# First loads on one DMA queue in pieces, the first attention's tables loaded in its first stage, the lambda vectors moved into the attention

## The chip, the cores and the metric

The kernel runs on one core of a Trainium2 chip, in one launch. Its time is device microseconds (us) of that core; the value that counts is the median of several runs. The engines are PE (matrix products, and PEld, its weight loads), DVE (vector), ACT (activation), POOL (GpSimd) and SP, which here only issues DMA transfers. Every engine works through its own instructions in order.

## What is computed

Two layers of a streaming encoder on 1024 tokens of width 1024, in float32. Layer 0 mixes tokens by latent attention, layer 1 by differential attention; each is followed by a normalisation and a SwiGLU block. The change touches the start of layer 0 and one scalar of layer 1:

```python
h = x @ w_in                                   # 1024 x 704: 384 + 256 + 64 columns
c_q, c_kv, k_rope = jnp.split(h, [384, 640], axis=-1)
c_q, c_kv = _rmsnorm(c_q, g_q), _rmsnorm(c_kv, g_kv)
q  = (c_q  @ w_uq ).reshape(b, s, 8, 128 + 64) # 8 heads: plain part, rotary part
kv = (c_kv @ w_ukv).reshape(b, s, 8, 128 + 128)
q_rope, k_rope = rope(q[..., 128:]), rope(k_rope)
logits = (q_nope . k_nope + q_rope . k_rope) * scale, masked by chunks of 64
o = softmax(logits) @ v
...
lam = exp(sum(lam_q1 * lam_k1)) - exp(sum(lam_q2 * lam_k2)) + lambda_init   # layer 1
o   = rmsnorm(o, g_sub) * (1 - lambda_init)                                 # layer 1
```

## The kernel before

**Precision.** Every matrix product is made of three passes on two rounded parts of each operand: hi x hi, hi x lo and lo x hi. So each operand that is loaded is first split: ACT copies it to the type float32r (the hi part, `A.copy`), and DVE or POOL subtracts that from the original (the lo part).

**First stage (pool a0).** `load_x(tb)` loads block tb of x, transposed, 128 x 1024 (512 KB), and splits it into xh and xl; `load_w_in(k)` does the same for rows k of the input weights, 128 x 704 (352 KB), into wih and wil, the lo part on DVE, or on POOL for k = 3, 5, 7. Block 0 of x comes in four pieces, block 1 in two, and the weights whole, in the order x 0, w 0, w 1, x 1, w 2 to w 7. `project` (L960) then multiplies blocks 0 and 1 together, k by k, six pairs of matmuls for each k: L970 writes hq (384 columns, the query latent) and L971 hk (320 columns, the key and value latent and the rotary key). Blocks 2 to 7 follow one at a time, three pairs for each k; there are three buffers for x, xh and xl, so a block's load waits for the block three before. `latents` (L974) squares and normalises a block (cve, crs, cn; it needs the gains gq and gk and the rotary table kt), and `turn_c` transposes cn on PE with the identity ident and splits it into c, ck_hi and ck_lo.

**Queues.** ident, x, the weights and all later loads are issued by SP and go to DMA queue q1. The rows gq and gk, the table kt, the vector g_sub and the four lambda vectors (each spread over 128 partitions by `bcast_row`) are issued by POOL and go to queue q0, at the beginning of the program.

**Lambda.** Behind the first stage, L1019 to L1032 scale g_sub and form the scalar nlam from the four vectors, in a small pool of its own, lam. Both are read by layer 1 only.

**First attention (pools a1...).** The tables ba (the mask), cos and sin, each 128 x 1024 (512 KB), are loaded when these pools open (L1040 to L1045). `q_rope`, `q_nope`, `k_nope` and `values` project two heads' rotary queries (qr), one head's queries (qn) and keys (kn) and two heads' values (v); `q_rope` multiplies its result by cos (L1059, qra) and by sin in four quarters (L1061, qrb), adds both on POOL (L1062) and splits the sum (ACT L1065, L1067; DVE L1066, L1068). `score_a` makes the scores s_a of a block of 128 queries in five passes (L217: three with kn and q, two with ck and the rotary queries) and DVE takes the row maximum (L220, mx_a). `attention` runs head by head and block by block; `at(slot, fn)` hangs a projection or a load on a block's slot.

**Order.** The program is written with pools and tiles, and a scheduler puts each engine's instructions into an order of its own before the kernel is built, by its own estimate of when each can run. So an instruction's place need not be that of its line.

## Time and profile before

Times of the kernel before, in us:

| | |
|---|---|
| median of 3 runs | 2333.69 |
| lowest and highest run | 2331.33, 2339.92 |
| span of the profiled execution | 2331.5 |
| first matmul of the program | 13.47 |
| first matmul of block 2 | 32.07 |
| first matmul of the attention's projections | 82.95 |
| PE busy, share of the span | 2254.7, 97% |

The profile gives no time of its own for the profiled execution beside its span, which lies within the range of the runs; nothing else is added to it. A row of a timeline has the start, the duration, the engine, the line of the kernel, the operation, the names that are written and read, the shape, a count where several are merged, and in brackets the idle time before it with what ended it. "hq L970 <- ACT wih L137: 13.5, 1, 13.5" is a wait: who waited, for whom, us in total, how often, the longest.

### The profile page before, as it was taken

How to read it: one execution, taken by the hardware profiler on the slowest of the kernel's cores; microseconds unless marked ns; L12 is line 12 of the kernel's file. 1: busy time of each engine (PE TensorE's matmuls, PEld its weight loads, DVE VectorE, ACT ScalarE, POOL GpSimd, SP SyncE). 2: the span in 40 equal slices, each digit the busy share in tenths (PEclk: the TensorE clock that was granted, in tenths of full speed). 3: DMA queues.
4: the chain of work that ended last, by engine and by line, in shares of the span. 5: the costliest groups of instructions: out<-in, count | busy, mean ns of one | idle time of the engine just before them, and what ended most of it. 6: DMA issues, size and time to landing. Idle time of an engine off the chain costs nothing. (4 is left out here: it accounts for less than half of the span.)

```text
span 2331.5 us, 31115 instructions
## 1 busy us (share of the span) xinstructions
PE 2254.7 (97%) x11410; PEld 1918.7 (82%) x11410; DVE 1556.9 (67%) x2876; ACT 1017.4 (44%) x2089; POOL 894.8 (38%) x706
## 2 busy tenths in 40 slices
PE   7899999999999999999999999979999999999997
PEld 7898997888888887888888898867788888887885
DVE  4567664596656667677576666666596656658777
ACT  4366664352333333444465656545342333324353
POOL 3233452014444445555432424222014444436564
PEclk9999999999999999999999999989999999999999
DMA  5112324344323238454220212153334323337353
GB/s 201 35 57 89 120 90 161 109 163 153 118 85 131 73 118 320 172 194 153 91 55 19 69 37 69 37 190 101 124 141 151 107 98 106 111 131 303 142 203 118
DMA packets 102490, 288.29 MB, mean 124 GB/s; under 512 B 7856, under 2 KB 30000, under 8 KB 91840
## 3 DMA queue, kind: packets, MB, share of 16 engines
q1 hardware_dynamic: 96480, 267.48, 32.4%
q0 software_dynamic: 5856, 18.81, 2.5%
q8 instruction: 90, 1.47, 0.3%
q14 instruction: 64, 0.52, 0.1%
HBM read 205.00 MB, written 77.07 MB: 121 GB/s over the span
## 5 line engine op out<-in xcount | busy, mean ns | idle before, releaser
L470 ACT CAST op_g<-gr 128x512 fp32r<-128x512 f32 x240 | 147.5, 622 | 410.7 <-PE gb L515 228.1
L471 POOL TENSOR_TENSOR op_g<-gr,op_g 128x512 fp32r<-128x512 f32 x104 | 145.9, 1408 | 303.0 <-DVE tmp L606 153.6
L471 DVE TENSOR_TENSOR op_h<-rh,op_h 128x512 fp32r<-128x512 f32 x154 | 161.4, 1078 | 69.9 <-ACT op_h L470 69.9
L515 PE MATMUL ga<-xh_m,op_g 128*128 128x512 f32 x512 | 168.0, 389 | 0.0
L470 ACT CAST op_h<-rh 128x512 fp32r<-128x512 f32 x154 | 92.9, 619 | 147.7 <-PE dx L783 37.2
L783 PE MATMUL dw<-op_w_t,op_h 128*128 128x512 f32 x660 | 151.4, 390 | 0.2 <-DVE op_h L471 0.2
L783 PEld LDWEIGHTS dw<-op_w_t,op_h 128*128 128x128 f32 x660 | 123.6, 188 | 26.1 <-DVE op_h L471 0.6
L223 ACT ACTIVATE l_b<-l_b,mx_b 128x256 f32<-128x256 f32 (+7 forms) x128 | 99.6, 778 | 76.0 <-DVE mx_b L220 74.3
L1269 POOL TENSOR_SCALAR l_b<-l_b,r_b,cst 128x128 f32<-128x128 f32 (+3 forms) x64 | 52.8, 825 | 204.0 <-DVE r_b L225 194.8
L471 POOL TENSOR_TENSOR op_w_t<-tt,op_w_t 128x512 fp32r<-128x512 f32 x66 | 98.7, 1499 | 78.7 <-ACT op_w_t L470 76.8
L783 PE MATMUL dx<-op_w_b,op_h 128*128 128x512 f32 x528 | 122.6, 391 | 5.9 <-ACT op_w_b L470 3.9
L783 PEld LDWEIGHTS dx<-op_w_b,op_h 128*128 128x128 f32 x528 | 98.4, 188 | 29.8 <-ACT op_w_b L470 4.7
L515 PE MATMUL gb<-t4h_f,op_g 128*128 128x512 f32 x352 | 115.8, 390 | 3.2 <-DVE tmp L598 3.2
L515 PE MATMUL gc<-b22h_f,op_g 128*128 128x512 f32 x352 | 115.6, 389 | 1.0 <-ACT op_g L470 1.0
L471 DVE TENSOR_TENSOR op_g<-gr,op_g 128x512 fp32r<-128x512 f32 x136 | 109.5, 806 | 9.0 <-ACT op_g L470 8.8
L515 PE MATMUL gc<-t1h_f,op_g 128*128 128x512 f32 x352 | 115.5, 389 | 0.0
L515 PE MATMUL gb<-t3h_f,op_g 128*128 128x512 f32 x352 | 115.2, 389 | 0.0
L515 PE MATMUL gb<-t2h_f,op_g 128*128 128x512 f32 x352 | 114.9, 389 | 0.0
L515 PEld LDWEIGHTS ga<-xh_m,op_g 128*128 128x128 f32 x512 | 96.1, 188 | 20.0
L471 POOL TENSOR_TENSOR op_g<-s,op_g 128x512 fp32r<-128x512 f32 x40 | 55.9, 1398 | 142.9 <-ACT op_g L470 142.9
L144 PE MATMUL bp<-xT_f,h_wb 128*128 128x512 f32 x256 | 103.0, 402 | 0.1
L146 PE MATMUL bp<-xT_f,l_wb 128*128 128x512 f32 x256 | 101.6, 397 | 0.0
(381 smaller groups left out, 6788.5 us busy)
## 6 DMA issues: line engine op xcount, KB each, us to landing
gr<-in_w_gu SPq DMA_DIRECT2D x44, 1024.0 KB, 6.6
rh<-h_dr SPq DMA_DIRECT2D x28, 1024.0 KB, 4.9
h_dr<-sh SPq DMA_DIRECT2D x22, 1024.0 KB, 4.9
h_dr<-hp SPq DMA_DIRECT2D x22, 768.0 KB, 4.1
tt<-in_w_dn SPq DMA_DIRECT2D x22, 512.0 KB, 7.6
rh<-h_dr SPq DMA_DIRECT2D x14, 768.0 KB, 4.4
z<-xs_dr SPq DMA_DIRECT2D x16, 512.0 KB, 10.0
rw_b<-in_w_dn SPq DMA_DIRECT2D x8, 1024.0 KB, 8.8
```

What stands on the lines that cost most here:

```text
L144: T.matmul(ps_out, lh, rh, start=(i == 0), stop=False)
L146: T.matmul(ps_out, ll, rh, start=False, stop=(i == n - 1))
L223: A.activation(l[:, :n], l[:, :n], AF.Exp, bias=mx, scale=-1.0, accum_out=sm)
L470: A.copy(hi, src)
L471: eng.tensor_tensor(lo, src, f32(hi), ALU.subtract)
L515: T.matmul(o, w[:, a, kc], x[b][:, k, :], start=(first and k == 0 and (a, b) == (0, 0)), stop=(k == 3 and a == 1), skip_group_check=True,)
L783: T.matmul(o, h[:, a, c], w[:, b_], start=(first and (a, b_) == (0, 0)), stop=(last and a == 1), skip_group_check=True,)
L1269: G.tensor_scalar(l1[:, :n], l1[:, :n], r1, nlam, ALU.mult, ALU.mult)
```

## The change

- The loads of x for blocks 0 and 1 and of the weights are issued in the order in which PE uses them: a quarter of x 0, w 0 in two parts (384 and 320 columns), a quarter of x 1, w 1, and then for each further quarter the pieces of x 0 and x 1 and two weights. `load_x` takes the number of the piece. The weights have five raw buffers instead of eight, and are split within `load_w_in`.
- ident, gq, gk and kt are issued by SP behind these loads. POOL issues no DMA at the start any more.
- The tiles ba, cos and sin move to the pool krp, which is open from the beginning, and are loaded when block 3's x is.
- The lambda vectors and their dot products get room in the tile `edge` (before, it was unused there). Their loads and that of g_sub (`load_late`) are hung on slot 10 of the first attention and the arithmetic (`make_late`) on slot 12.

The sums, the splits and the matmuls are the same; two pieces of a weight are now split in two instructions, and x 1 in four instead of two.

The scheduler sets where these end up. On SP, the first issues of the program (x_0 and x_1 are blocks 0 and 1 of x, wraw0 to wraw7 the weights by k) stood so before:

```order
L102 DMA ident_61<-in_c_ident 128x128
L937 DMA x_0_113<-in_xt 128x256 x4
L133 DMA wraw0_130<-in_w_in_a 128x704
L133 DMA wraw1_136<-in_w_in_a 128x704
L937 DMA x_1_140<-in_xt 128x512 x2
L133 DMA wraw2_151<-in_w_in_a 128x704
L133 DMA wraw3_157<-in_w_in_a 128x704
L133 DMA wraw4_163<-in_w_in_a 128x704
```

and stand so now:

```order
L940 DMA x_0_117<-in_xt 128x256
L949 DMA wraw0_123<-in_w_in_a 128x384
L949 DMA wraw0_123<-in_w_in_a 128x320
L940 DMA x_1_132<-in_xt 128x256
L949 DMA wraw1_138<-in_w_in_a 128x704
L940 DMA x_0_117<-in_xt 128x256
L940 DMA x_1_132<-in_xt 128x256
L949 DMA wraw2_150<-in_w_in_a 128x704
L949 DMA wraw3_156<-in_w_in_a 128x704
```

The first weights stood behind ident and four pieces of x and now stand behind one piece, and half of them counts as a load of its own. Behind these rows come the other pieces of x, w 4 to w 7, ident, gq, gk, kt, x 2, cos, sin, x 3, ba and x 4, then the first attention's first weights, g_sub and the four lambda vectors (places 30 to 34) and x 5 to x 7: although the lambda vectors are written into slot 10 of the attention, the scheduler has put them into the first stage, their arithmetic too, on DVE behind the split of x 4.

On DVE, at the end of the first stage and the start of the attention (c11 and ck_lo are the lo parts of the last block's latents, ql0_0 and kn1_0 those of head 0's first queries and keys, vl0_0 and vl0_1 of the first values, qra0_0 and qrb0_0 the rotary products of the first half, qr0_0 and qr1_0 their lo parts) stood before:

```order
L1004 TENSOR_TENSOR c11_104<-cp7_0_863,c01_102 128x4x128
L1004 TENSOR_TENSOR ck_lo_109<-cp7_4_870,ck_hi_108 128x2x128
L1097 TENSOR_TENSOR ql0_0_964<-qn0_0_953,qh0_0_963 128x512
L1111 TENSOR_TENSOR kn1_0_968<-kn0_0_969,kn0_0_967 128x512
L1083 TENSOR_TENSOR vl0_0_1034<-v0_0_1026,vh0_0_1033 128x256
L1059 TENSOR_TENSOR qra0_0_933<-qr0_0_923,cos_913 128x512
L1083 TENSOR_TENSOR vl0_1_1045<-v0_1_1037,vh0_1_1044 128x256
L1061 TENSOR_TENSOR qrb0_0_934<-qr0_0_923,sin_915 32x512 x4
L1097 TENSOR_TENSOR ql0_1_1083<-qn0_1_1072,qh0_1_1082 128x512
L1066 TENSOR_TENSOR qr0_0_0_941<-qra0_0_933,qr0_0_0_941 64x512
L1068 TENSOR_TENSOR qr1_0_0_942<-qra0_0_933,qr1_0_0_942 64x512
```

and stand now:

```order
L1069 TENSOR_TENSOR qra0_0_920<-qr0_0_910,cos_110 128x512
L1071 TENSOR_TENSOR qrb0_0_921<-qr0_0_910,sin_111 32x512 x4
L1013 TENSOR_TENSOR c11_103<-cp7_0_878,c01_101 128x4x128
L1013 TENSOR_TENSOR ck_lo_108<-cp7_4_885,ck_hi_107 128x2x128
L1107 TENSOR_TENSOR ql0_0_951<-qn0_0_940,qh0_0_950 128x512
L1121 TENSOR_TENSOR kn1_0_955<-kn0_0_956,kn0_0_954 128x512
L1076 TENSOR_TENSOR qr0_0_0_928<-qra0_0_920,qr0_0_0_928 64x512
L1078 TENSOR_TENSOR qr1_0_0_929<-qra0_0_920,qr1_0_0_929 64x512
L1093 TENSOR_TENSOR vl0_0_1021<-v0_0_1013,vh0_0_1020 128x256
L1093 TENSOR_TENSOR vl0_1_1032<-v0_1_1024,vh0_1_1031 128x256
```

The two rotary products moved from behind the first values to the front, ahead of the last block's split, and the lo parts of the rotary queries to the place before the values. PE's order moved with it: the first values now stand ahead of the first scores; the rotary passes of the scores of query blocks 0 and 1 stand behind the rotary projection of the second half, and all passes of block 2 behind that half's keys; before, both came only behind head 1's first query projection. From block 3's scores on PE's order is the old one, but for a few neighbours that change places much later.

```diff
--- before.py
+++ after.py
@@ -83,7 +83,7 @@
     ones = cp.tile([P, P], F32, tag="ones", name="ones")
     cst = cp.tile([P, 48], F32, tag="cst", name="cst")
     edge = ctx.enter_context(tc.tile_pool(name="edge", bufs=1, side="right"))
-    edge.tile([P, 504], F32, tag="edge", name="edge")
+    late = edge.tile([P, 504], F32, tag="edge", name="edge")
     wp = ctx.enter_context(tc.tile_pool(name="wp", bufs=3))
     big = ctx.enter_context(tc.tile_pool(name="big", bufs=5))
     ps, ps_bufs, ps_stack = None, None, None
@@ -99,7 +99,6 @@
     banks("ps0", PS_BUFS_A)
     dr = ctx.enter_context(tc.tile_pool(name="dr", bufs=1, space=DRAM))
 
-    nc.sync.dma_start(ident, c_ident)
     mhalf = cst[:, 0:2]
     V.memset(mhalf, -0.5)
     eps_rms = cst[:, 8:9]
@@ -148,9 +147,9 @@
     def tr(ps_out, in_):
         T.transpose(ps_out, in_, ident)
 
-    def bcast_row(pool, src, n, name, tag):
+    def bcast_row(pool, src, n, name, tag, eng=None):
         t = pool.tile([P, n], F32, tag=tag, name=name, bufs=1)
-        nc.gpsimd.dma_start(t, src.partition_broadcast(P))
+        (eng or nc.gpsimd).dma_start(t, src.partition_broadcast(P))
         return t
 
     def behind(i, j):
@@ -917,6 +916,7 @@
     krp = ast.enter_context(tc.tile_pool(name="krp", bufs=1))
     lat2 = [big_tile("ck_hi"), krp.tile([P, 2, S], F32R, tag="cklo", name="ck_lo")]
     kr1, kr2 = lat2[0][:, 1], lat2[1][:, 1]
+    ba, cos, sin = (krp.tile([P, S], F32, tag=t, name=t) for t in ("ba", "cos", "sin"))
 
     def lat(p, k, t0, n):
 
@@ -927,35 +927,44 @@
     with tc.tile_pool(name="a0", bufs=2, side="right") as pool:
         xs, win = {}, []
 
-        def load_x(tb, n=1):
-
-            xt = pool.tile([P, D], F32, tag="x", name=f"x_{tb}", bufs=3)
-            xh = pool.tile([P, D], F32R, tag="xh", name=f"xh{tb}", bufs=3)
-            xl = pool.tile([P, D], F32R, tag="xl", name=f"xl{tb}", bufs=3)
-            for i in range(n):
-                c = slice(i * D // n, (i + 1) * D // n)
-                nc.sync.dma_start(xt[:, c], xt_in[tb, :, c])
-                A.copy(xh[:, c], xt[:, c])
-                V.tensor_tensor(xl[:, c], xt[:, c], f32(xh[:, c]), ALU.subtract)
-            xs[tb] = (xh, xl)
+        def load_x(tb, i=0, n=1):
+
+            if tb not in xs:
+                xs[tb] = (
+                    pool.tile([P, D], F32R, tag="xh", name=f"xh{tb}", bufs=3),
+                    pool.tile([P, D], F32R, tag="xl", name=f"xl{tb}", bufs=3),
+                    pool.tile([P, D], F32, tag="x", name=f"x_{tb}", bufs=3),
+                )
+            xh, xl, xt = xs[tb]
+            c = slice(i * D // n, (i + 1) * D // n)
+            nc.sync.dma_start(xt[:, c], xt_in[tb, :, c])
+            A.copy(xh[:, c], xt[:, c])
+            V.tensor_tensor(xl[:, c], xt[:, c], f32(xh[:, c]), ALU.subtract)
 
         def load_w_in(k):
             hi = pool.tile([P, 704], F32R, tag=f"wih{k}", name=f"wih{k}", bufs=1)
             lo = pool.tile([P, 704], F32R, tag=f"wil{k}", name=f"wil{k}", bufs=1)
-            raw = pool.tile([P, 704], F32, tag="wraw", name=f"wraw{k}", bufs=8)
-            load_w(w_in_a[k], 704, f"win{k}", hi, lo, G if k > 2 and k % 2 else V, raw)
+            raw = pool.tile([P, 704], F32, tag="wraw", name=f"wraw{k}", bufs=5)
+            for c in (slice(0, 384), slice(384, 704)) if k == 0 else (slice(0, 704),):
+                nc.sync.dma_start(raw[:, c], w_in_a[k][:, c])
+                A.copy(hi[:, c], raw[:, c])
+                (G if k > 2 and k % 2 else V).tensor_tensor(lo[:, c], raw[:, c], f32(hi[:, c]), ALU.subtract)
             win.append((hi, lo))
 
-        load_x(0, 4)
+        load_x(0, 0, 4)
         load_w_in(0)
+        load_x(1, 0, 4)
         load_w_in(1)
-        load_x(1, 2)
-        for k in range(2, KD):
-            load_w_in(k)
-        gq = bcast_row(pool, g_q, RQ, "gq", "gq")
-        gk = bcast_row(pool, g_kv, RKV, "gk", "gk")
+        for i in range(1, 4):
+            load_x(0, i, 4)
+            load_x(1, i, 4)
+            load_w_in(2 * i)
+            load_w_in(2 * i + 1)
+        nc.sync.dma_start(ident, c_ident)
+        gq = bcast_row(pool, g_q, RQ, "gq", "gq", nc.sync)
+        gk = bcast_row(pool, g_kv, RKV, "gk", "gk", nc.sync)
         kt = pool.tile([P, NTB, P], F32, tag="kt", name="kt", bufs=1)
-        nc.gpsimd.dma_start(kt, c_krope)
+        nc.sync.dma_start(kt, c_krope)
 
         def project(tbs):
             ms = [(ps_m(f"hq{tb}"), ps_t(f"hk{tb}")) for tb in tbs]
@@ -963,7 +972,7 @@
                 kc = slice(k * P, (k + 1) * P)
                 wh, wl = win[k]
                 for tb, (hq, hk) in zip(tbs, ms):
-                    xh, xl = xs[tb]
+                    xh, xl, _ = xs[tb]
                     for lh, w, st, sp_ in (
                         (xh, wh, k == 0, False), (xh, wl, False, False), (xl, wh, False, k == KD - 1)
                     ):
@@ -1008,6 +1017,9 @@
             for tb in tbs:
                 if tb > 1:
                     load_x(tb)
+                if tb == 3:
+                    for t, src in ((cos, c_cos), (sin, c_sin), (ba, c_bias_a)):
+                        nc.sync.dma_start(t, src)
             ms = project(tbs)
             for tb, cn in done:
                 turn_c(tb, cn)
@@ -1017,13 +1029,18 @@
 
 
     gs = cst[:, 16:17]
-    nc.gpsimd.dma_start(gs, g_sub)
-    V.tensor_scalar(gs, gs, 1.0 - LAMBDA_INIT, None, ALU.mult)
+    nlam = cst[:, 24:25]
     V.memset(ones, 1.0 / P)
-    nlam = cst[:, 24:25]
-    with tc.tile_pool(name="lam", bufs=1) as pool:
-        lv = [bcast_row(pool, t, 64, f"lv{i}", f"lv{i}") for i, t in enumerate((lam_q1, lam_k1, lam_q2, lam_k2))]
-        dots = pool.tile([P, 2], F32, tag="dots", name="dots")
+    lv = [late[:, 64 * i:64 * i + 64] for i in range(4)]
+    dots = late[:, 256:258]
+
+    def load_late():
+        nc.sync.dma_start(gs, g_sub)
+        for t, src in zip(lv, (lam_q1, lam_k1, lam_q2, lam_k2)):
+            nc.sync.dma_start(t, src.partition_broadcast(P))
+
+    def make_late():
+        V.tensor_scalar(gs, gs, 1.0 - LAMBDA_INIT, None, ALU.mult)
         for i in range(2):
             V.tensor_tensor(lv[2 * i], lv[2 * i], lv[2 * i + 1], ALU.mult)
             V.tensor_reduce(dots[:, i:i + 1], lv[2 * i], mybir.AxisListType.X, ALU.add)
@@ -1031,18 +1048,11 @@
         V.tensor_tensor(nlam, dots[:, 1:2], dots[:, 0:1], ALU.subtract)
         V.tensor_scalar(nlam, nlam, -LAMBDA_INIT, None, ALU.add)
 
-
     with ast as st:
         pool = st.enter_context(tc.tile_pool(name="a1", bufs=2, reuse_waits="tile"))
         vp = st.enter_context(tc.tile_pool(name="a1v", bufs=12, side="right", reuse_waits="tile"))
         lp = st.enter_context(tc.tile_pool(name="a1l", bufs=4, side="right", reuse_waits="tile"))
         ptp = st.enter_context(tc.tile_pool(name="a1p", bufs=5, side="right", reuse_waits="tile"))
-        ba = pool.tile([P, S], F32, tag="ba", name="ba", bufs=1)
-        nc.sync.dma_start(ba, c_bias_a)
-        cos = pool.tile([P, S], F32, tag="cos", name="cos", bufs=1)
-        nc.sync.dma_start(cos, c_cos)
-        sin = pool.tile([P, S], F32, tag="sin", name="sin", bufs=1)
-        nc.sync.dma_start(sin, c_sin)
         vt, qr, qn, kn, wts, lt, pts = {}, {}, {}, {}, {}, {}, {}
 
         def q_rope(pr, hf):
@@ -1163,6 +1173,8 @@
             at(b + (6 if h < H - 1 else 4), q_nope, h, 1)
             at(b + (7 if h < H - 1 else 5), k_nope, h, 1)
         at(8 * H - 20, split_wo, H - 1)
+        at(10, load_late)
+        at(12, make_late)
         attention(score_a, turn_a, mix_a, fill, 2, (0, 0))
 
     banks("ps2", PS_BUFS)
```

## The prediction

> **What bounds the kernel now.** I read the page first, for what the span is made of.
>
> ```profile
> span 2331.5 us, 31115 instructions
> PE 2254.7 (97%) x11410; PEld 1918.7 (82%) x11410; DVE 1556.9 (67%) x2876; ACT 1017.4 (44%) x2089; POOL 894.8 (38%) x706
> ```
>
> PE, the matmul engine, is busy 97% of the span: time can only be won where PE stands still or where its clock is low, 77 us in all. The change works in the first attention's first stage (latents) and at its start, so I cut that stretch into stages, by busy time per engine: before the first matmul; the projection of blocks 0 and 1; blocks 2 to 7; the start of the attention. After the time of each engine come the granted clock, the DMA share and GB/s.
>
> ```profile
> 0.00:13.47 13.47, 0.00 (x1) 0.00 (x1) 1.96 (x8) 3.68 (x6) 4.62 (x12) 1.00 0.79 226
> 13.47:32.07 18.60, 18.60 (x97) 18.17 (x97) 11.33 (x15) 10.31 (x15) 9.31 (x5) 1.00 0.73 277
> 32.07:82.26 50.19, 50.19 (x326) 50.09 (x325) 24.64 (x80) 15.99 (x46) 6.37 (x8) 1.00 0.20 70
> 82.26:112.31 30.05, 24.14 (x116) 19.39 (x116) 20.88 (x47) 13.07 (x31) 8.81 (x8) 0.94 0.20 68
> ```
>
> PE has two holes: 13.47 us at the start and 30.05 - 24.14 = 5.91 us at the transition, where the clock also falls to 0.94. Between them, from 13.47 to 82.26, there is none: whatever is won at the start is carried through to 82.26. The waits of PE up to 125 us name who ended each hole.
>
> ```profile
> PE hq L970 <- ACT wih L137: 13.5, 1, 13.5
> PE s_a L217 <- DVE mx_a L220: 4.2, 3, 2.8
> PE s_a L217 <- ACT kn L1110: 1.7, 1, 1.7
> ```
>
> **The start.** The timeline from 0, SP's DMA issues, ACT and PE:
>
> ```profile
> 0.73 0.38 SPq L102 DMA_DIRECT2D ident<-in_c_ident  x1
> 1.17 1.85 SPq L937 DMA_DIRECT2D x<-in_xt  x4
> 3.06 1.15 SPq L133 DMA_DIRECT2D wraw<-in_w_in_a  x2
> 3.92 0.40 ACT L938 CAST xh<-x 128x256 fp32r<-128x256 f32 x1 [1.91 <-DMA x<-in_xt]
> 12.64 0.78 ACT L137 CAST wih<-wraw 128x704 fp32r<-128x704 f32 x1 [3.31 <-DMA wraw<-in_w_in_a]
> 13.47 0.69 PE L970 MATMUL hq<-wih,xh 128*128 128x384 f32 x1 [13.47 <-ACT wih L137]
> 19.83 0.34 PE L970 MATMUL hq<-wil,xh 128*128 128x384 f32 x1
> 32.07 0.34 PE L970 MATMUL hq<-wih,xh 128*128 128x384 f32 x1
> ```
>
> The first quarter of x is there at 3.92, the first weights only at 12.64. The DMA issues by line (count, KB, us from issue to landing):
>
> ```profile
> ident<-in_c_ident SPq DMA_DIRECT2D x1, 64.0 KB, 1.8
> x<-in_xt SPq DMA_DIRECT2D x4, 128.0 KB, 5.5
> wraw<-in_w_in_a SPq DMA_DIRECT2D x8, 352.0 KB, 9.5
> ```
>
> The queues from 2 to 6 us, and below the dots from 14 to 22 us (packets, MB, share of 16 engines):
>
> ```profile
> q0 software_dynamic: 90, 0.29, 42.0%
> q1 hardware_dynamic: 459, 0.39, 32.5%
> ...
> q1 hardware_dynamic: 1174, 3.33, 103.5%
> ```
>
> From 2 to 6 us GpSimd's queue q0 (gq, gk, kt, g_sub, the lambda vectors) took more of the engines than SP's q1. Per full engine share q1's rows of 1 KB ran at 0.39 MB / (0.325 x 4 us) = 300 GB/s; later, alone, its rows of 2.8 KB ran at 3.33 MB / 8 us = 416 GB/s.
>
> The change puts ahead of the first matmul only one x piece and the left part of w0. x0's piece is issued where ident was, at 0.73, w0's at 0.73 + 1.85/4 = 1.2. Landing costs between ident's 1.8 us and the 2.75 us of the first x piece (1.17 to 3.92): 3.0 to 4.0 us. The cast of 384 columns lies between 0.40 (256) and 0.78 (704), about 0.5. PE starts at 3.5 to 4.5; I take 4.2, nearer to ident, since q0 is silent now. The far bound is the pieces' median of 5.5 us: 1.2 + 5.5 + 0.5 = 7.2. **First term: 13.47 - 4.2 = 9.3 us**, at worst 6.3.
>
> Is PE then fed? Its 48 pairs of matmuls took 19.83 - 13.47 = 6.36 us for the first 10, slow, then (32.07 - 19.83) / 38 = 0.322 each. The weights of one k serve 6 pairs: 3.8 us slow, 1.93 us later, so k = 7 is reached at 4.2 + 6.36 + 32 x 0.322 = 20.9. SP issues 17 pieces at about 0.5 us (1.85/4, 1.15/2), the last by 9, an estimate. The bytes: 1.05 MB of x at 300 GB/s is 3.5 us, 2.88 MB of weights at 416 is 6.9; from 1.7 on, all is there by 13 to 14, 7 us early. The tightest place is k = 0 and 1, where casts follow the landings closely: I charge 0.3 us. The deeper split of w and the five raw buffers instead of eight ask w5 to w7 to wait for DVE's splits of k = 0 to 2, done by about 9, when SP gets there anyway. Block 2's x comes behind ident, gq, gk and kt, 5.37 MB in all: 1.7 + 3.5 + 4.32/0.416 = 15.6 and a cast of 1.05 (0.40 + 768 columns x 0.38/448), against PE's need at 23.1. Cost nothing; cover 5 us or more. So blocks 0 and 1 end at 4.2 + 6.36 + 38 x 0.322 + 0.3 = 23.1 instead of 32.07: **9.0 us (6.0 to 9.9)**.
>
> The slow first pairs are the clock's: from rows 13.47 and 19.83 they cost 0.636 us each against 0.322. The Trainium skill, "TensorE: Matmul & The Clock Gate", Part 1, What's actually happening, states a free-running window of 3.4 us, so warming takes 3.4 to 6.8 us after a start; this trace's 6.36 fits its long end. By that page the sum would gain up to (6.36 - 3.4) x (1 - 0.322/0.636) = 1.5 us more, an estimate; I keep the row's 6.36.
>
> **Lambda, g_sub and the tables.** The five small loads (0.13 MB) stand at places 30 to 34 of SP's queue, with cos, sin and ba ahead. On DVE eight short instructions now stand behind the split of block 4's x and ahead of the latents of block 2, which can't start before PE ends that block, at 23.1 + 50.19/6 = 31.5. The old trace shows that cover as DVE's idle time:
>
> ```profile
> 32.11 1.23 DVE L939 TENSOR_TENSOR xl<-x,xh 128x1024 fp32r<-128x1024 f32 x1 [6.04 <-PE hq L970]
> ```
>
> The lambda rows need 8.9 MB landed, 1.7 + 3.5 + 7.9/0.416 = 24 us, so 7 us of cover: nothing. Without it, each us of lateness would shift the latents, which PE needs only a block (8.4 us) later.
>
> **The transition.** PE, DVE, POOL, ACT and SP:
>
> ```profile
> 51.45 0.42 SPq L1045 DMA_DIRECT2D sin<-in_c_sin  x1
> 84.69 0.39 PE L145 MATMUL qr<-c,h_wa 128*128 128x512 f32 x1
> 84.91 0.40 PE L146 MATMUL qr<-c,l_wa 128*128 128x512 f32 x1
> 85.82 0.48 DVE L993 SCALAR_TENSOR_TENSOR cn<-hk,crs,gk 128x256 f32<-128x256 f32 x1
> 89.83 0.69 DVE L1004 TENSOR_TENSOR c<-cp,c 128x512 fp32r<-128x512 f32 x1 [3.54 <-ACT c L1003]
> 91.11 0.50 PE L217 MATMUL s_a<-kn,qh 128*128 128x128 f32 x2 [1.71 <-ACT kn L1110]
> 91.37 0.68 DVE L1111 TENSOR_TENSOR kn<-kn,kn 128x512 fp32r<-128x512 f32 x1
> 93.28 0.68 DVE L1059 TENSOR_TENSOR qra<-qr,cos 128x512 f32<-128x512 f32 x1
> 94.57 2.79 DVE L1061 TENSOR_TENSOR qrb<-qr,sin 32x512 f32<-32x512 f32 x4
> 97.50 1.29 POOL L1062 TENSOR_TENSOR qra<-qra,qrb 128x512 f32<-128x512 f32 x1 [12.94 <-DVE qrb L1061]
> 98.81 0.62 ACT L1065 CAST qr<-qra 64x512 fp32r<-64x512 f32 x1 [0.38 <-POOL qra L1062]
> 99.47 0.69 DVE L1066 TENSOR_TENSOR qr<-qra,qr 64x512 fp32r<-64x512 f32 x1 [0.31 <-ACT qr L1065]
> 104.86 0.79 PE L217 MATMUL s_a<-kn,qh 128*128 128x384 f32 x2 [2.83 <-DVE mx_a L220]
> 108.67 0.27 PE L149 MATMUL pt_a<-ident,l_a 128*128 128x128 f32 x1
> 114.59 0.34 PE L217 MATMUL s_a<-kn,ql 128*128 128x384 f32 x1
> 114.76 0.33 PE L217 MATMUL s_a<-ck_hi,qr 128*128 128x384 f32 x1
> ```
>
> The tables were not late: sin was issued at 51.45, and its product ran at 94.57. What was late is DVE's place for the rotary products: head 0's raw product is complete at 85.3, DVE idles 3.54 us until 89.83, and only at 93.28 does it multiply. In the new order the products (0.68 + 2.79 = 3.47 us) stand just ahead of that c split: they fill the idle time, and the rotary part is ready at about 89.8 + 1.29 + 0.62 + 0.69 = 92.8 on the old clock, behind the k split (92.05), instead of 100. PE's order follows: the first values come ahead of the scores (the hole of 1.71 shrinks to two of about 0.45), the rotary scores of blocks 0 and 1 right behind the second half's rotary projection, and block 2's scores ahead of head 1's projection, so DVE can free the score banks while PE projects; the 2.83 hole goes. With it goes the slow clock behind it: from 104.86 to 108.67 ten matmuls took 3.81 us; at the later spacings (0.17 for 384 columns, 0.22 for 512) they would take 2.0, so 1.8 us. Walking the new order with the old durations, 1.2 us stay: the two halves of the first hole, and about 0.3 on DVE's row maximum of block 3, then behind the second half's rotary split. Sum: 5.91 + 1.8 = 7.7, less 1.2: **second term 6.5 us**. Bounds: 7.7 above; below, a loss of 1.2, if ACT's two casts of 0.62, now ahead of the values' casts, are waited for and nothing else gains.
>
> The rest of the program keeps its order but for three swaps of neighbours. Both gains shift it as a whole, since nothing there waits on an absolute time.
>
> **Sum.** 9.0 + 6.5 = 15.5 us off the profiled 2331.5: 2316.0. The median of the runs, 2333.7, lies 2.2 above that span, so I forecast 2318.2. A measurement of this kernel can tell about 0.5%, 11.7 us, from no change: under 2322.0 is faster.
>
> **Rivals.** *Start only.* PE's new order meets another wait (a score bank, ACT's casts, POOL's split of a 1024-column weight in between) and the transition gains nothing: 2333.7 - 9.0 = 2324.7. For it: PE's program is in order, and one late producer stalls all. Against it: each producer I followed has 0.3 us or more. Chance 0.14.
>
> *The start is fed poorly.* PE starts early, then waits for pieces with its clock low, and keeps only 5 us: 2333.7 - 11.5 = 2322.2, on the border. For it: both queues together moved only (0.29 + 0.39) MB / 4 us = 170 GB/s from 2 to 6 us; were the 1 KB rows to blame and not q0, 3.9 MB would take until 25. Against it: the 300 GB/s per share. Chance 0.13.
>
> *The queue serves pieces one at a time*, the slower side. Each piece would pay ident's 1.8 us, less 0.2 for its own bytes. Block 5's x is the 35th DMA, 9.44 MB in: 0.73 + 35 x 1.6 + 9.44/0.416 + 1.05 = 80.5, against 32.07 + 3 x 8.37 = 57.2 now: 23.3 late, less 6.5, so 2350.5. It decides from 1.1 us a piece on (24.5 + 35 x 1.1 = 57.2 + 6.5, no gain left; 1.5 for slower by 0.5%). Against it: in 14 to 22 us q1 moved nine weight pieces' worth in 8 us. The Trainium skill, "DMA: Bandwidth & Descriptors", section Measured, says to batch DMAs to 1 MiB or more, and Anatomy of one DMA gives 2.0 us of fixed cost each; taken in series that rule would make it slower still, and the 416 GB/s row speaks against taking it so. Chance 0.04.
>
> *It does not do what it says*: the weights' arrival depends on something other than what is queued, and DVE's place was not the hold-up: 2333.7. Chance 0.03.
>
> **Numbers.** The forecast has 0.66. Faster: 0.66 and half of the poorly fed case, 0.72; same: the other half, start only, no effect, 0.24; slower 0.04. Range: down to 9.9 + 7.7 + 1.5 = 19.1 (2314.6) and 2 more for the scatter of the runs, 2312; up past start only, with its start at 6.0 (2327.7), 2328.
>
> **What would show it.** Right: the first matmul at about 4, the first one on block 2 at 23 with no gap between; DVE's cos product directly behind the last cn; no PE wait of over 1 us on the row maximum; the stage that ended at 112.31 ended some 15 us earlier. Wrong: weight casts in the first 20 us that wait for DMA while PE idles; DVE waiting at the lambda product past 31; a first block-5 matmul later than 50; or a PE gap of 2 us and more at the first scores.

## The result, and the profile after

| | before | after |
|---|---|---|
| median, us | 2332.51 (4 runs, 2329.69 to 2339.92) | 2318.48 (4 runs, 2317.24 to 2320.63) |
| span of the profiled execution | 2331.5 | 2315.5 |
| first matmul | 13.47 | 4.25 |
| first matmul of block 2 | 32.07 | 23.78 |
| end of the stage of the transition | 112.31 | 97.89 |

The ratio is 0.9939, with a 95% interval of 0.9924 to 0.9953: faster by 0.6%, and the forecast of 2318.2 lies 0.3 us from the median. The forecast span was 2316.0, and 2315.5 was measured.

The changed kernel's page has the same matmuls in a shorter span; PE's busy time is 1.3 us less:

```profile
span 2315.5 us, 31126 instructions
PE 2253.4 (97%) x11410; PEld 1918.7 (83%) x11410; DVE 1560.1 (67%) x2879; ACT 1018.5 (44%) x2092; POOL 891.9 (39%) x698
```

The same four stages as in the prediction, by busy time per engine of the changed kernel:

```profile
0.00:4.25 4.25, 0.00 (x0) 0.00 (x0) 0.69 (x5) 2.20 (x3) 0.19 (x4) 1.00 0.49 127
4.25:23.78 19.53, 18.74 (x97) 18.30 (x97) 11.14 (x15) 10.10 (x20) 5.90 (x3) 1.00 0.99 360
23.78:74.09 50.31, 50.31 (x326) 50.16 (x325) 28.23 (x86) 18.46 (x47) 11.48 (x10) 1.00 0.25 83
74.09:97.89 23.80, 22.01 (x116) 18.19 (x114) 21.25 (x47) 12.59 (x31) 7.49 (x7) 1.00 0.16 55
```

The first stage fell from 13.47 to 4.25, the second rose from 18.60 to 19.53, the third is unchanged (50.19 and 50.31), the last fell from 30.05 to 23.80, and its clock is 1.00 where it was 0.94. The DMA share of the second stage is 0.99 instead of 0.73: the loads now run under the matmuls instead of ahead of them.

What PE waited for up to 125 us (total, times, longest):

```profile
PE hq L979 <- ACT wih L950: 4.3, 1, 4.3
PE s_a L216 <- DVE mx_a L219: 0.9, 1, 0.9
PE hk L980 <- ACT wih L950: 0.8, 1, 0.8
PE s_a L216 <- ACT kn L1120: 0.4, 1, 0.4
```

The 13.5, 4.2 and 1.7 of before have become 4.3, 0.9 and 0.4. The start, in ACT's and PE's rows:

```profile
3.02 0.40 ACT L941 CAST xh<-x 128x256 fp32r<-128x256 f32 x1 [1.01 <-DMA x<-in_xt]
3.69 0.51 ACT L950 CAST wih<-wraw 128x384 fp32r<-128x384 f32 x1 [0.26 <-DMA wraw<-in_w_in_a]
5.22 0.46 ACT L950 CAST wih<-wraw 128x320 fp32r<-128x320 f32 x1 [1.02 <-DMA wraw<-in_w_in_a]
4.25 0.69 PE L979 MATMUL hq<-wih,xh 128*128 128x384 f32 x1 [4.25 <-ACT wih L950]
5.73 0.63 PE L980 MATMUL hk<-wih,xh 128*128 128x320 f32 x1 [0.79 <-ACT wih L950]
11.86 0.33 PE L979 MATMUL hq<-wih,xl 128*128 128x384 f32 x1
23.78 0.34 PE L979 MATMUL hq<-wih,xh 128*128 128x384 f32 x1
```

PE begins with the left part of weight 0, stands 0.79 us for its right part, and runs slowly until 11.86. The transition, DVE's rows and three of PE's:

```profile
77.52 0.48 DVE L1002 SCALAR_TENSOR_TENSOR cn<-hk,crs,gk 128x256 f32<-128x256 f32 x1
77.91 0.68 DVE L1069 TENSOR_TENSOR qra<-qr,cos 128x512 f32<-128x512 f32 x1
78.60 2.79 DVE L1071 TENSOR_TENSOR qrb<-qr,sin 32x512 f32<-32x512 f32 x4
81.53 0.69 DVE L1013 TENSOR_TENSOR c<-cp,c 128x512 fp32r<-128x512 f32 x1
90.74 0.34 PE L216 MATMUL s_a<-kn,ql 128*128 128x384 f32 x1
90.92 0.35 PE L216 MATMUL s_a<-ck_hi,qr 128*128 128x384 f32 x1
93.19 2.13 DVE L1076 TENSOR_TENSOR qr<-qra,qr 64x512 fp32r<-64x512 f32 x1
97.05 0.56 PE L216 MATMUL s_a<-kn,qh 128*128 128x320 f32 x2 [0.89 <-DVE mx_a L219]
```

The products with the tables stand directly behind the last cn and end where the c split begins, so DVE's idle 3.54 us are gone. The scores of block 2 follow each other at 0.18 us (90.74, 90.92), the full clock.

### The profile page after: what moved, and what is told of

It is laid out like the page before. It is cut to its first block, busy times and chain, and to the rows that moved or that the text cites. A ratio compares the mean times of both kernels' runs of the same rounds, so it can differ in the third digit from the quotient of the medians.

```text
span 2315.5 us, 31126 instructions
## 1 busy us (share of the span) xinstructions
PE 2253.4 (97%) x11410; PEld 1918.7 (83%) x11410; DVE 1560.1 (67%) x2879; ACT 1018.5 (44%) x2092; POOL 891.9 (39%) x698
```

## Experiments

My theory: two gains that don't depend on each other. The start gains from a silent second queue and from pieces in the order of use; the transition gains because DVE multiplies with the tables ahead of the c split, not because the tables arrive earlier. The rivals: one part of the start's edits does it all; the transition gains from the earlier arrival or the earlier start. One thing no run separates: DVE's order and PE's order moved together.

All kernels are compared at the same instructions: the first matmul; the first of block 2; Q, the first matmul of the rotary queries (82.98 in the trace of before; the 82.95 given ahead is 0.03 too low); S, the time from Q to the fourth transposition pt_a, where the stage of the transition ends; and A, the time from Q to the start of the last score product of the first attention, the same work in each. In S lie the same 108 matmuls in every kernel but e2 and e4, which have 13 more there (starred). The medians are of timed runs, and the ratio is to the kernel before in the same series.

| kernel | first | block 2 | Q | S | A | span | median | ratio (95%) |
|---|---|---|---|---|---|---|---|---|
| before | 13.47 | 32.07 | 82.98 | 29.34 | 276.9 | 2331.5 | 2334.03 beside e1 to e4 | |
| changed | 4.25 | 23.78 | 74.67 | 23.22 | 269.6 | 2315.5 | 2318.48 | 0.9939 (0.9924 to 0.9953) |
| changed, again | 4.65 | 23.68 | 74.6 | 23.23 | 269.6 | 2318.0 | 2319.84 | 0.9940 (0.9926 to 0.9954) |
| e1 queue alone | 9.13 | 26.69 | 77.64 | 28.03 | 273.5 | 2330.7 | 2329.40 | 0.9982 (0.9969 to 0.9994) |
| e2 order and pieces alone | 4.48 | 27.50 | 78.40 | 25.19* | 267.8 | 2325.8 | 2325.84 | 0.9962 (0.9951 to 0.9972) |
| e3 tables late | 4.75 | 23.46 | 74.35 | 28.78 | 276.0 | 2326.3 | 2329.99 | 0.9983 (0.9972 to 0.9994) |
| e4 tables alone | 13.21 | 30.73 | 81.64 | 25.19* | 267.8 | 2318.1 | 2322.16 | 0.9952 (0.9933 to 0.9970) |
| e5 lambda back | 4.26 | 25.13 | 76.0 | 23.24 | 270.0 | 2317.5 | 2318.58 | 0.9937 (0.9924 to 0.9950) |
| e6 x whole | 5.86 | 26.53 | 77.4 | 23.25 | 269.8 | 2321.8 | 2323.58 (1 run) | |
| e7 dummies ahead | 4.63 | 22.30 | 73.6 | 23.22 | 270.7 | 2314.2 | 2315.93 | 0.9926 (0.9913 to 0.9939) |
| e7, again | 4.54 | 21.82 | 72.7 | 23.25 | 269.6 | 2314.1 | 2315.51 | 0.9929 (0.9917 to 0.9941) |
| e8 dummies, one sum on POOL | 4.54 | 23.40 | 74.3 | 23.23 | 270.8 | 2313.5 | 2313.98 | 0.9919 (0.9907 to 0.9932) |

**S and A.** S is the transition itself. A goes on for some 245 us behind it, and there steps of about 1.1 us come and go that are no part of the change. One of them, in the kernel before and, at the same work, in the changed kernel:

```profile
179.65 1.56 POOL L138 TENSOR_TENSOR l_wa<-r_wa,h_wa 128x640 fp32r<-128x640 f32 x1 [0.64 <-DMA wo_dr<-l_pwo]
179.66 2.10 DVE L1068 TENSOR_TENSOR qr<-qra,qr 64x512 fp32r<-64x512 f32 x1
165.22 0.69 DVE L1078 TENSOR_TENSOR qr<-qra,qr 64x512 fp32r<-64x512 f32 x1
165.30 2.04 POOL L137 TENSOR_TENSOR l_wa<-r_wa,h_wa 128x640 fp32r<-128x640 f32 x1 [0.73 <-POOL l_a L1137]
```

The engine that started second ended late. In the kernel before that was DVE, by 0.01 us; the split of the values stood behind it, and PE waited 0.86 us for that. So of A's 7.3 us 6.1 are the stage, and 1.1 is this step.

**e1: the second queue silent, nothing else.** The kernel before with

```
-        gq = bcast_row(pool, g_q, RQ, "gq", "gq")
+        gq = bcast_row(pool, g_q, RQ, "gq", "gq", nc.sync)
-        nc.gpsimd.dma_start(kt, c_krope)
+        nc.sync.dma_start(kt, c_krope)
```

and the same for gk, g_sub and the lambda vectors.

> The kernel before, with one edit: the loads of g_q, g_kv, the key rotary table, g_sub and the four lambda vectors are issued by SP behind the first loads, so that nothing else moves while x and the first weights land. Sizes and order of the pieces stay as before; the products with the rotary tables stay late on VectorE. Main theory (the second queue took about a third of the early bandwidth, and the order of the pieces adds to it): the first matmul, which was at 13.47 us, comes behind 0.92 MB of the first queue at some 240 GB/s, at 6 to 7.5 us; block 2, which began at 32.07 us, begins at 25.5 to 27.5; the stage of the transition keeps its 30.05 us (29.5 to 30.6). Span about 2326 (2324 to 2328) against 2331.5. Rival 1 (the gain of the start is all order and pieces, the second queue is harmless): first matmul later than 11, block 2 later than 30, span 2330 to 2332. Rival 2 (what gained at the transition was only that everything came earlier): the transition takes 24 to 25 us here too.

Block 2 came 5.4 us earlier, as expected (26.69), but the first matmul only at 9.13, later than the 6 to 7.5 I gave: 4.3 us of the gain are the first matmul's, and 1.0 comes from a slow first phase of PE that lasted 4.03 us here instead of 6.36, which varies by itself (see e4). The DMA queue from 2 to 6 us (packets, MB, share of 16 engines):

```profile
q1 hardware_dynamic: 761, 0.85, 81.9%
```

On top of these 0.85 MB, 0.61 more moved from 6 to 8 us (305 GB/s), and weight 0 had its cast only at 8.30, although ident, x and weight 0 are 0.95 MB: the pieces behind it in the queue shared the engines with it. Against the rival: the second queue did matter. The transition is a small miss: S fell by 1.3 us, where I expected no change. The products still stand behind the c split, but the scheduler moved the sine products ahead of the values' second low half, and the rotary scores of the first two blocks ahead of head 1's projection on PE; the largest row-max wait was 1.39 us instead of 2.83, and no slow clock followed. The rest of A's 3.4 us are two of the DVE steps above (179.66 and 248.72 in the kernel before), which e1 doesn't have.

**e2: order and pieces, the second queue busy.** The changed kernel with `nc.gpsimd` for gq, gk, kt, g_sub and lambda, and weight 7 first loaded into the space of ba.

> The changed kernel, but the loads of g_q, g_kv, the key rotary table, g_sub and the lambda vectors are issued by GpSimd on its own queue at the very start, as before; the pieces and their order stay as in the changed kernel (one raw tile more, in the bias table's space, so that the last weight isn't held up). Main theory: the first queue gets about 165 GB/s instead of 240 while the second one is busy, until about 12 us. First matmul at 4.5 to 6 us, but the matmuls of the first four steps wait for weights; block 2 at 25 to 28 us (23.78 in the changed kernel); the transition takes 23.8 us (23.3 to 24.5) since VectorE's order is that of the changed kernel. Span 2317 to 2320. Rival (order and pieces alone are the gain): block 2 at 23.5 to 24.3, span 2315 to 2316.

The queues from 2 to 6 us, and PE's waits up to 125 us:

```profile
q1 hardware_dynamic: 460, 0.52, 46.2%
q0 software_dynamic: 81, 0.25, 33.8%
```

```profile
PE hq L979 <- ACT wih L950: 5.3, 2, 4.5
PE hq L979 <- ACT xh L941: 1.2, 1, 1.2
...
PE hk L980 <- ACT wih L950: 0.9, 1, 0.9
```

In the same 4 us the changed kernel's q1 moved 0.95 MB, this one's 0.52. PE starts as early, at 4.48, and then starves: block 2 at 27.50, within my 25 to 28. The rival (23.5 to 24.3) is out. Order alone brings 4.6 us, the silent queue alone 5.4 with its shorter slow phase, both 8.3. A has the whole gain of the transition, and more (9.1 us against 7.3): e2 and e4 have the products ahead of the c split like the changed kernel, but otherwise nearly the same third order, in which 13 matmuls of the values and the output come within S. The time, 2325.84, is above my 2317 to 2320; where that went stands below.

**e3: the tables late again.** The changed kernel with the three loads in the first attention's pool.

```
-                if tb == 3:
-                    for t, src in ((cos, c_cos), (sin, c_sin), (ba, c_bias_a)):
-                        nc.sync.dma_start(t, src)
+        cos = pool.tile([P, S], F32, tag="cos", name="cos", bufs=1)
+        nc.sync.dma_start(cos, c_cos)
...
```

> The changed kernel, with one part undone: the bias, cosine and sine tables are loaded in the first attention's pool, as before. They are on the chip long before their use, but VectorE's order goes back to that of before (products with the tables behind the c split, ql and kl). Main theory (the transition's gain is VectorE's order): block 2 at 23.8 (23.5 to 24.1) as in the changed kernel; the transition, 23.80 us there, takes 30 (29.3 to 30.6), with a wait of TensorE of 4.5 to 6 us for the row max of the first scores and a slow clock behind it. Span 2321.7 (2321 to 2323). Rival (the transition gains from the tables' earlier arrival, or because the whole start is earlier): landing of the tables ends a wait on VectorE, or the transition stays at 23.8 and the span at 2315.5.

SP's issue of cos, and DVE's rows:

```profile
34.05 0.42 SPq L1055 DMA_DIRECT2D cos<-in_c_cos  x1
81.21 0.69 DVE L1012 TENSOR_TENSOR c<-cp,c 128x512 fp32r<-128x512 f32 x1 [3.54 <-ACT c L1011]
83.34 0.68 DVE L1071 TENSOR_TENSOR qra<-qr,cos 128x512 f32<-128x512 f32 x1
84.76 2.79 DVE L1073 TENSOR_TENSOR qrb<-qr,sin 32x512 f32<-32x512 f32 x4
```

cos was issued at 34.05 and landed 5.7 us later, over 40 us ahead of its use at 83.34, and nothing waited for it. Yet DVE idles 3.54 us ahead of the c split again, and S is back at 28.78: of its gain of 6.1 us 5.6 are lost (of A's 7.3, 6.4), at the same early start. PE waited 4.2 us for row maxima, a little under the 4.5 to 6 I gave, and no slow clock followed. So the gain goes with the order of the engines, and not with the arrival of the data. That DVE's place leads and PE's order follows is read from the rows. Since the place of the tables and of their loads is the only edit, what it changes is presumably the scheduler's estimate of when the products can run; that estimate itself is not on record.

**e4: the tables early, nothing else.** The kernel before with the three loads at block 3, and weights 5 to 7 first loaded into the tables' space.

> The kernel before, with one part of the change: the bias, cosine and sine tables are loaded in the first stage behind block 3's x (the last three raw weight tiles lie in their space first, so that the start stays as it was). VectorE then has the products with the tables ahead of the c split. Main theory (two gains that do not depend on each other): first matmul and block 2 as before, 13.47 and 32.07 (within 0.5); the transition takes 23.8 (23.3 to 24.6) instead of 30.05 us; span 2325.3 (2324.5 to 2326.5). Rival (the transition's gain hangs on the earlier start): the transition takes 28 us or more, span 2330 or more.

S is 25.19, and about 23.6 without the 13 further matmuls, which follow each other at 0.12 us; A fell by 9.1 us from a start at 13.21: the transition doesn't need the earlier start, and the rival is out. Two numbers were off. A's gain is 2.9 us more than my 6.2: 1.1 is the DVE step at 179.66, which e4 doesn't have, and the rest lies in the third order, where it stays open. And block 2 began 1.3 us earlier than before, although the first matmul came only 0.26 earlier: the slow first phase of PE lasted 3.99 us (13.21 to 17.20) instead of 6.36.

**e5: lambda at the start again.** The changed kernel with g_sub and lambda as before.

> The changed kernel, with one part undone: g_sub and the four lambda vectors are loaded by GpSimd at the start, as before, and the arithmetic on them stands on VectorE among the casts of the first stage. All else as in the changed kernel. Main theory (their bytes are few, 0.13 MB after spreading to 128 partitions, but they share the DMA engines in the first microseconds): first matmul 4.3 to 5.2 us, block 2 at 23.8 to 25.3 (23.78 in the changed kernel), the first product of the rotary queries at 74.7 to 76.2, and the transition as in the changed kernel. A loss of 0 to 1.5 us. Rival 1 (VectorE, waiting in order for a lambda vector that has not landed, holds up the low halves of the weights): block 2 later than 26 with waits of TensorE for VectorE in the first steps. Rival 2 (any use of the second queue costs what all its loads cost): block 2 at 27 or later, as with the other loads of the second queue at the start (27.5).

The row in which it shows:

```profile
7.67 0.69 PE L979 MATMUL hq<-wih,xh 128*128 128x384 f32 x1 [1.53 <-ACT xh L941]
```

The second queue moved 0.06 MB from 2 to 6 us and took 25.2% of the engines' time for it, and block 1's first piece came late; block 2 came at 25.13, 1.4 us later. VectorE held nothing up. So moving lambda isn't free of effect, as the prediction had it: in this one execution it is 1.4 of the start's 8.3 us; the slow first phase, with that gap in it, lasted 9.1 us. The medians (2318.58 and 2319.84) can't tell 1.4 us.

**e6: x of blocks 0 and 1 whole.** The changed kernel with `load_x(0); load_w_in(0); load_x(1)` and then weights 1 to 7, the last three first loaded into the space of the tables.

> The changed kernel with x of blocks 0 and 1 loaded whole (0.52 MB each) instead of in four pieces each: x of block 0, weight 0 in its two pieces, x of block 1, then weights 1 to 7 (the last three into the tables' space first, so that nothing holds them up). One queue, order of use, no pieces of x. It tells what the pieces bring of the 3 us by which the changed kernel's start is ahead of the kernel in which only the second queue was silent. Theory (the first matmul waits for all bytes ahead of its own): it comes behind 0.72 MB at some 240 to 330 GB/s instead of 0.33, at 5.7 to 7 us; weight 1 comes behind 1.74 MB at 8.5 to 9.5 us, where TensorE waits again; block 2 at 25 to 26.5 us (first rotary product at 75.9 to 77.4), against 23.8 and 26.7. Rival (pieces cost as much in number as they bring in order): block 2 at 24 or earlier.

First matmul at 5.86, inside its range; block 2 at 26.53, at the upper end of the 25 to 26.5. So the pieces of x bring 2.75 us, by one execution each (26.53 - 23.78), about as much as the changed kernel is ahead of e1 (2.9).

**e7: dummy products ahead.** The changed kernel with

```
+        warm = pool.tile([P, P], F32, tag="warm", name="warm", bufs=1)
+        V.memset(warm, 0.0)
+        pw = ps_s("pwarm")
+        for i in range(8):
+            T.matmul(pw[:, :128], warm, warm, start=True, stop=True)
```

> The changed kernel, and ahead of it eight dummy products of a 128x128 tile of zeros on TensorE, into a bank that is written over later, from about 1 us until the first weights are there. Nothing of the reference is left out. Theory (the first steps are slow because TensorE's clock is low at first, for 7.6 us of work in the changed kernel, 4.0 and 3.8 us in two others): with the dummies the real matmuls run at the full clock from 5 to 7 us on instead of 11.86; the weights then become the limit (their casts end at 7.7, 9.8, 12.5 ... 16.2 us), so that block 2 begins at 22.0 to 22.8 us instead of 23.78, a gain of 1 to 1.8 us that no later stage gives back. Rival 1 (the first steps are bound by the weights' arrival, the clock is beside the point): block 2 at 23.5 or later. Rival 2 (the clock falls back in the gaps of the first steps, each under 1 us): matmuls slow again after 6 us, block 2 at 23.5 or later.

> The changed kernel with eight dummy products ahead, a second time, as the measure for the kernel below: 2315.4 to 2317 us in single runs, first rotary product at 73.4 to 73.9 us.

PE's rows in the second of these executions (the trace counts each dummy twice):

```profile
1.11 3.79 PE L934 MATMUL pwarm<-warm 128*128 128x128 f32 x16 [1.11 <-DVE warm L931]
4.54 0.67 PE L985 MATMUL hq<-wih,xh 128*128 128x384 f32 x1
5.60 0.52 PE L985 MATMUL hq<-wih,xl 128*128 128x384 f32 x1
6.61 0.45 PE L985 MATMUL hq<-wih,xh 128*128 128x384 f32 x1 [0.48 <-ACT xh L947]
7.04 0.34 PE L985 MATMUL hq<-wil,xh 128*128 128x384 f32 x1
```

Full speed from 7.04 and 7.60 instead of 11.86, block 2 at 21.82 and 22.30: 1.4 to 2.0 us earlier (Q at 72.7 in the second, ahead of the 73.4 to 73.9 I gave). The times are lower by more than that (2315.93 and 2315.51 against 2319.84 and 2318.48, no run of either above 2317.78), and what the start doesn't explain of it stays open. The clock at the start was worth about what I estimated. In e8, with the same start, full speed came only at 10.51.

**Where e1, e2 and e3 lost time later.** By Q and A they are 8.7, 13.7 and 9.5 us ahead of before; the medians give 4.6, 8.2 and 4.0. From the last product of layer 2's output projection (zp_a) to the last dw they need 648.3, 650.0 and 645.9 us, where before needs 642.1, the changed kernel 641.2 and e4 641.4. At the start of layer 2's experts stand, on DVE and PE, in the changed kernel:

```profile
1672.37 1.29 DVE L470 TENSOR_TENSOR t1l_f<-xr_m,t1h_f 128x512 fp32r<-128x512 f32 x2 [0.31 <-ACT t1h_f L469]
1675.87 0.69 DVE L545 TENSOR_TENSOR gr<-gr 128x512 f32<-128x512 f32 x1 [2.20 <-DMA gr<-in_w_gu]
```

in e3:

```profile
1682.32 0.69 DVE L545 TENSOR_TENSOR gr<-gr 128x512 f32<-128x512 f32 x1 [4.31 <-DMA gr<-in_w_gu]
1682.93 0.69 DVE L470 TENSOR_TENSOR t1l_f<-xr_m,t1h_f 128x512 fp32r<-128x512 f32 x1
1700.52 1.22 PE L514 MATMUL ga<-xh_m,op_gp 128*128 128x512 f32 x2 [3.74 <-DVE op_gp L470]
```

and in the changed kernel's second execution:

```profile
1676.56 0.69 DVE L545 TENSOR_TENSOR gr<-gr 128x512 f32<-128x512 f32 x1 [3.08 <-DMA gr<-in_w_gu]
1692.81 0.50 PE L514 MATMUL gc<-b22h_f,op_g 128*128 128x512 f32 x1 [2.63 <-ACT op_g L469]
1694.82 1.05 PE L514 MATMUL ga<-xh_m,op_gp 128*128 128x512 f32 x2
1697.75 0.39 PE L514 MATMUL gc<-t1h_f,op_g 128*128 128x512 f32 x1
```

In e2 and e3 the scheduler put the sum gr, which waits for its DMA, ahead of two low halves of t1 that stand ahead of it in the changed kernel. DVE idles 3.8 and 4.3 us, PE later 3.7, and its clock is low behind that. So edits in the first 100 us changed an order at 1680 us; that this order costs the time is read from the rows, and only e8, below, acts on it. And the place varies without any edit: in two executions of the changed kernel gr landed 6.1 and 7.2 us after its issue, PE stood 1.59 and 2.63 us, only after the longer wait did the clock fall, and the stretch took 641.2 and 644.1 us. e1 has the old order here and a wait of 2.6 us with a slow clock behind it; its other loss, and e2's, is a PE wait of 3.7 and 3.9 us for DVE's z near 2285 us, where before had 1.8. Why z came later there stays open.

**e0: the changed kernel again**, the measure for e5 and e7.

> The changed kernel itself, again, on the chip and beside the runs of the two kernels below: the measure for them. First matmul at 4.2 to 4.8 us, first product of the rotary queries at 74.4 to 74.9, the first expert matmul (ga) at 453 to 455; time 2315 to 2322 in single runs.

**e8: that sum off DVE.** e7 with

```
-                V.tensor_tensor(a21, a21, a22, ALU.add)
+                (G if layer and not n else V).tensor_tensor(a21, a21, a22, ALU.add)
```

> The changed kernel with the eight dummy products, and in the second expert layer the first sum of two weight quarters (a21 + a22 of unit 0) on GpSimd instead of VectorE. In three earlier kernels VectorE stood 3.2 to 4.3 us at that sum, at about 1680 us, waiting for the weights' DMA, and TensorE then waited 2.6 to 3.7 us for an operand that VectorE made behind it, with a slow clock after the wait. Theory (a wait at the head of VectorE's queue, far from the change, eats what the start gained): VectorE makes the low halves of t1 and b22 in that time, TensorE's wait for the operand of gc (2.0 us with the dummies alone) falls to under 0.7, and the time falls by 1 to 3 us against the kernel with the dummies. Rival (TensorE waits there for other operands as well, or GpSimd's slower sum of 1.3 us delays unit 0 by as much): no difference beyond 0.5 us.

PE's wait for gc fell from 2.2 to 1.2 us, not under 0.7: DVE's next sum now waited 1.97 us for POOL's. The median is 1.5 us lower than e7's beside it, but the runs overlap (2310.95 to 2315.24, and 2314.79 to 2317.78), so that e8 beats e7 is likely and not settled. Every run of e8 was below every run of the changed kernel (2316.77 at least): both kernels of the study are beaten, by 0.8% and by about 0.2%.

## Why the prediction was right, step by step

*The first matmul at 4.2, a gain of 9.3.* Measured 4.25 and 9.22.

*Block 2 at 23.1, a gain of 9.0.* Measured 23.78 and 8.29. Two terms were mis-sized. The feed at k = 0 and 1, charged 0.3, cost 0.79: the right part of weight 0 probably shared the engines with the pieces behind it, as weight 0 did in e1. And the slow phase, taken over as 6.36, lasted 7.61 with that stall in it. That phase isn't a property of the kernel: it lasted 6.36 and 3.99 us with the same start (before and e4), and with the same dummies full speed came at 7.04, 7.60 and 10.51. So 0.7 us of error is less than what its scatter allows. The cover was thinner than worked out: SP issued the last weight by 11.1 instead of 9, its cast began at 15.46 where all was to be there by 13 to 14 (the terms given, 1.7, 3.5 and 6.9, make 12.1), and block 2's x was cast at 19.77 instead of 15.6; PE still waited for none of them. The Trainium skill, "TensorE: Matmul & The Clock Gate", Part 1, What's actually happening, says that the window is free-running and that the same kernel shows different numbers of slow matmuls in different runs; the three executions with dummies (7.04, 7.60, 10.51) agree. One to two of its windows of 3.4 us would be 3.4 to 6.8 us, an estimate from that figure: e4's 3.99 and the 6.36 of before lie in it, the changed kernel's 7.61 only without its stall, and e5's 9.1 and e8's 9.4 (from the first dummy at 1.11) lie outside.

*Lambda at no cost.* Its new place costs nothing, as forecast: its products ran on DVE from 29.7 to 33.6 us without a wait for DMA or of PE. Its old place cost 1.4 us at the start (e5), which the prediction had within the start's sum without naming it.

*The transition, 6.5.* The stage fell by 6.25. The mechanism, the products ahead of the c split and not earlier data or an earlier start, is shown by e3 and e4. PE's waits in it are 0.35, 0.39, 0.16 and 0.89 us, together 1.8 where I left 1.2: the row maximum of block 3 was 0.89 instead of 0.3, since DVE's rotary split ahead of it took 2.13 us (row 93.19) instead of the 0.69 of the old trace. POOL was splitting a 1024-column weight:

```profile
92.38 2.40 POOL L137 TENSOR_TENSOR l_pwo<-r_pwo,h_pwo 128x1024 fp32r<-128x1024 f32 x1
```

The prediction named this split among what a rival could rest on, and charged nothing for it. The twelve traces hold 192 of these DVE splits: the 25 that started while POOL was within such an operation on two tiles took 1.50 to 2.13 us and ended 0.54 to 0.55 us behind POOL, the other 167 took 0.68 to 1.08. No run moved POOL's split away. The matmuls in turn took 22.0 us, 2.1 less than before, where I had 1.8.

*Sum 15.5, and the rest keeps its order.* At 97.89 the kernel is 14.4 us ahead, and 14.0 to 15.7 at all later places; the span is 16.0 shorter. The last 1.6 us aren't the change's: steps come and go behind the transition, the DVE step of 1.1 us in A among them, and the second execution of the changed kernel has a span of 2318.0 with the same first 98 us. The forecast also started from a median of 2333.7, which with a fourth run became 2332.51, so that the medians differ by 14.0 us and not by 15.5. So that the median came out within 0.3 us of the forecast is partly luck; a fair reading is two terms of 8.3 and 6.3 us, each right to 0.7.

*The rivals.* Start only, poorly fed, in series: all out, by S (6.1 us less), by one PE wait of 0.79 us at the start, and by the last weight's cast at 15.46; no effect at all is out by the ratio. But e2 shows that the poorly fed case was near: with the second queue busy it would have been just that.

## What to carry to other kernels

When a wait is put down to data that come late, look at when they were issued and landed: here the tables had been on the chip for 40 us, and what was late was the consumer's place in its engine's queue. Where a scheduler sets the order, an early load is also an input to it: read the whole new order, far behind the edit too, and compare kernels stage by stage, since here the last 640 us took back up to 9 us of what an early stage had won; and compare over the same short stretch of work, since A, some 245 us longer than S, added steps of its own. At a start, load in pieces in the order of use on one queue and keep the other silent: alone, either brought 4 to 5 of the 8.3 us, since what is needed first still shared the DMA engines with bytes needed later.

## What the runs showed of the hardware

- Pieces queued behind a piece share the DMA engines with it. In e1 weight 0 ends at 0.95 MB in the order of issue, but landed when about 1.5 MB had moved (17, 222, 204 and 305 GB/s in the four stretches of 2 us up to 8 us).
- Two queues at once moved less: 0.77 MB from 2 to 6 us in e2, against 0.95 MB by one queue in the changed kernel and 0.85 in e1.
- Behind the same PE gap the clock fell in some executions and not in others, so the length of the gap alone doesn't decide it. One gap of 1.95 us, ahead of dx near 880 and near 2090 us, stands 24 times in the twelve traces: behind 8 of them the matmuls went from 0.23 to 0.43 us apart, 0.6 to 1.5 us after the gap's end and for some eight matmuls, behind 16 they did not. In the changed kernel (16 matmuls in 3.92 us) and in e2 (19 in 6.22):

```profile
2088.82 3.92 PE L782 MATMUL dx<-op_w_b,op_h 128*128 128x512 f32 x16 [1.95 <-ACT op_w_b L469]
2093.97 6.22 PE L782 MATMUL dx<-op_w_b,op_h 128*128 128x512 f32 x19 [1.95 <-ACT op_w_b L469]
```

  After the gap of 2.63 us at 1692.81 the matmuls likewise kept 0.23 us for a microsecond and then took 0.43 us each until 1697.38; gaps of 1.59 and 2.2 us at that place brought none. The Trainium skill, "TensorE: Matmul & The Clock Gate", HAM oscillation, speaks of gaps over 3.4 us; here 1.95, 2.63 and 2.83 did it, and the measurement decides.
- DVE's split and POOL's, both on two tiles, held each other up: 2.10 us for DVE's 64x512 split that started 0.01 us behind POOL's, 0.69 us for the one that started 0.08 us ahead, and then 2.04 us for POOL's instead of 1.56.
- The granted clock of the profile reads 1.00 in the slow first phase, where a 384-column matmul takes 0.52 us instead of 0.34: that phase is seen in the durations alone.
